# Eight experts in a two-layer MLP on one core: taking the layers two experts at a time, and storing one result in thirteen small transfers

## The chip, the core and the metric

The kernel runs on one core of one Trainium2 chip. The core has a matrix engine (TensorE, "PE" in the profile, with a weight-load side "PEld"), a vector engine (VectorE, "DVE"), a scalar engine (ScalarE, "ACT"), GpSimd ("POOL") and a sync engine ("SP"). Sixteen DMA engines move data between the chip's main memory (HBM) and the core's on-chip memories; transfers can be issued from POOL (they run in the queue that the profile calls q0) or from SP (q1). The metric is the device time of one execution in microseconds (us), smaller being better. The profile is of one execution; the times are those of several.

## The reference

```
x  : 8 experts x 256 rows x 512          (float32)
w1 : 8 experts x 512 x 2048
w2 : 8 experts x 2048 x 512

h   = relu(x @ w1)        # per expert, 256 x 2048
out = h @ w2              # per expert, 256 x 512, float32
```

There are 64 MiB of float32 weights, each used once; x and the result have 4 MiB each.

## The kernel before

The program is written by hand, engine by engine; each engine runs its own list in order, and semaphores are the only order between engines.

**Loads.** POOL issues the weight loads (`load_w1`, `load_w2`), which turn float32 into bf16 on the way. One load brings a whole weight matrix of one expert, 2 MiB as bf16. There are two buffers for each layer, `w1_sb[e % 2]` and `w2_sb[e % 2]`; a load into a buffer waits until TensorE is through with the expert two before (`s_h` counts blocks of the first layer, `s_o` output halves of the second). The order in the queue is w1(0), half of x, w2(0), w1(1), w2(1), w1(2), w2(2) and so on. The last, w2(7), goes in two parts: the first 9 of its 16 chunks (`CUT = 9`) and then the other 7. The other half of x comes by SP in four transfers.

**The start.** ACT and DVE cast and reorder x, TensorE transposes it, ACT and DVE copy the result out, and DVE gives each expert its 256 columns in one of two buffers `xe` (`give_xe`).

**An expert.** The first layer is four blocks (`q`) of 16 matmuls (L230) of 256 columns into two PSUM buffers `ph`; ACT takes the even blocks and DVE the odd ones, applying relu and writing `ht` in bf16 (L188, L200). The second layer is 32 matmuls of 512 columns (L247): 16 chunks (`kt`) for each of the two halves of the result, into `po[0]` and `po[1]`. DVE and ACT copy one half each to `o_sb` (L204, L190). There is one pair of `po`. TensorE's loop of four turns holds two experts, each with its first layer and then its second.

**Signals to TensorE.** SP waits for every weight load in the order of the queue and then adds to `t_w`, from which TensorE takes one at the head of each layer, and one at chunk 9 of the second (L98 to L103).

**Stores.** The result is stored at the end of the queues. Behind all weights POOL issues results 0 to 2 in one transfer (L146) and result 3 in three, of 36, 36 and 56 partitions (L149, `CUTS`). A partition of one result is 4 KB in one piece, here called a row; a result has 128 rows. SP, having waited for the last weight (L103), issues results 4 to 6 in one transfer (L106), waits for the last two copies, and issues result 7 (L109).

Of the kernel before, what the change touches and what calls it, by code (L numbers as in the profile page):

```python
# [9 lines left out]
def kernel(  # L10
# [7 lines left out]
    nc = tc.nc  # L18
    P = 128
    bf = mybir.dt.bfloat16  # L20
    f32 = mybir.dt.float32
    relu = mybir.ActivationFunctionType.Relu

    E, C, H = x.shape
    F = w1.shape[2]
    MT = C // P
    KT1 = H // P
    KT2 = F // P
    FB = 4
    NQ = KT2 // FB  # L30
    G = E // 2
    J = G * MT
    KH = KT1 // 2
    CUT = 9
    CUTS = (0, 36, 72, 128)

    w1_r = w1.rearrange("e (p kt) n -> e p kt n", p=P)
    w2_r = w2.rearrange("e (p kt) n -> e p kt n", p=P)
    out_r = out.rearrange("e (p mt) n -> p e mt n", p=P)
# [6 lines left out]
    x_f = nc.alloc_sbuf_tensor("x_f", [P, J, H], f32)  # L46
    x_c = nc.alloc_sbuf_tensor("x_c", [P, J, H], bf)
    x_b = nc.alloc_sbuf_tensor("x_b", [P, J, KH, P], bf)
    xt = [nc.alloc_sbuf_tensor(f"xt{g}", [P, KT1, MT, G * P], bf) for g in range(2)]
    xe = [nc.alloc_sbuf_tensor(f"xe{b}", [P, KT1, MT, P], bf) for b in range(2)]  # L50
    w1_sb = [nc.alloc_sbuf_tensor(f"w1_sb{b}", [P, KT1, F], bf) for b in range(2)]
    w2_sb = [nc.alloc_sbuf_tensor(f"w2_sb{b}", [P, KT2, H], bf) for b in range(2)]
    ht = [nc.alloc_sbuf_tensor(f"ht_sb{b}", [P, KT2, C], bf) for b in range(2)]
    o_sb = nc.alloc_sbuf_tensor("out_sb", [P, E, MT, H], f32)
    identity = nc.alloc_sbuf_tensor("identity", [P, P], bf)
    ph = [nc.alloc_psum_tensor(f"pt_h{b}", [P, FB, C], f32) for b in range(2)]
    po = [nc.alloc_psum_tensor(f"pt_o{m}", [P, H], f32) for m in range(MT)]
    pt = [nc.alloc_psum_tensor(f"pt_tr{b}", [P, J, P], bf) for b in range(2)]

    sem = nc.alloc_semaphore  # L60
    s_x = [sem(f"s_x{g}") for g in range(2)]
    s_out = [sem(f"s_out{i}") for i in range(3)]


    def load_x(e):
        nc.sync.dma_start(
            x_f[:, e * MT:(e + 1) * MT], x[e].rearrange("(p m) k -> p m k", m=MT)
        ).then_inc(s_x[0], 16)

    with tc.tile_critical(no_gpsimd_drain=True):  # L70
        for e in range(G // 2):
            load_x(e)
    tc.close()
    tc.compile()  # L74

    s_w1 = [sem(f"s_w1_{e}") for e in range(E)]
    s_w2 = [sem(f"s_w2_{e}") for e in range(E)]
    s_w2b = sem("s_w2b")
    s_id = sem("s_id")
    s_act = sem("s_act")  # L80
    s_dve = sem("s_dve")
    s_tr = sem("s_tr")
    s_h = sem("s_h")
    s_o = sem("s_o")
    t_xb = sem("t_xb")
    t_pt = [sem(f"t_pt{b}") for b in range(2)]
    t_xe = sem("t_xe")
    t_w = sem("t_w")
    t_ha = sem("t_ha")
    t_hb = sem("t_hb")  # L90

    sp, pool, act, dve, pe = nc.sync, nc.gpsimd, nc.scalar, nc.vector, nc.tensor


    for e in range(G // 2, G):
        load_x(e)
    for e in range(E):
        sp.wait_ge(s_w1[e], 16).then_inc(t_w, 1)  # L98
        if e < E - 1:
            sp.wait_ge(s_w2[e], 16).then_inc(t_w, 2)  # L100
        else:
            sp.wait_ge(s_w2[e], 16).then_inc(t_w, 1)
            sp.wait_ge(s_w2b, 16).then_inc(t_w, 1)  # L103
    sp.wait_ge(s_act, E - 1)
    sp.wait_ge(s_dve, E - 1)
    sp.dma_start(out_r[:, G:E - 1], o_sb[:, G:E - 1]).then_inc(s_out[1], 16)  # L106
# [5 lines left out]
    def load_w1(e):  # L112
        pool.dma_start(w1_sb[e % 2][:], w1_r[e]).then_inc(s_w1[e], 16)  # L113

    def load_w2(e):
        if e < E - 1:
            pool.dma_start(w2_sb[e % 2][:], w2_r[e]).then_inc(s_w2[e], 16)  # L117
        else:
            b = w2_sb[e % 2]
            pool.dma_start(b[:, :CUT], w2_r[e, :, :CUT]).then_inc(s_w2[e], 16)  # L120
            pool.dma_start(b[:, CUT:], w2_r[e, :, CUT:]).then_inc(s_w2b, 16)

    load_w1(0)
    pool.dma_start(x_c[:], x_rows).then_inc(s_x[1], 16)
    load_w2(0)
    pool.memset(identity[:], 0.0).then_inc(s_id, 1)
    pool.wait_ge(s_id, 1)
    pool.affine_select(
# [5 lines left out]
        pattern=[[-1, P]],  # L134
        channel_multiplier=1,
    ).then_inc(s_id, 1)
    load_w1(1)
    load_w2(1)
    for e in range(2, E):
        pool.wait_ge(s_h, NQ * (e - 1))  # L140
        load_w1(e)
        pool.wait_ge(s_o, MT * (e - 1))
        load_w2(e)
    pool.wait_ge(s_act, G)
    pool.wait_ge(s_dve, G)
    pool.dma_start(out_r[:, :G - 1], o_sb[:, :G - 1]).then_inc(s_out[0], 16)  # L146

    for p0, p1 in zip(CUTS, CUTS[1:]):
        pool.dma_start(out_r[p0:p1, G - 1], o_sb[p0:p1, G - 1]).then_inc(s_out[0], 16)  # L149
    pool.drain()  # L150


    def take_x(eng, half):

        js = slice(half * J // 2, (half + 1) * J // 2)
        copy = act.copy if eng is act else dve.tensor_copy
        for g, src in enumerate((x_f, x_c)):
            eng.wait_ge(s_x[g], 16 * (1 if g else G))  # L160
            for k in range(0, KT1, KH):
                r = (g * KT1 + k) // KH
                if r:
                    eng.wait_ge(s_tr, KH * r)
                copy(  # L165
                    x_b[:, js],
                    src[:, js].rearrange("p j (q t) -> p j t q", t=KT1)[:, :, k:k + KH],
                ).then_inc(t_xb, 1)
                eng.wait_ge(s_tr, KH * r + half + 1)
                copy(  # L170
                    xt[g][:, k + half].rearrange(
                        "p m (q l) -> p l m q" if g else "p m (l q) -> p l m q", l=G
                    ),
                    pt[half][:].rearrange("p (l m) q -> p l m q", m=MT),
                ).then_inc(t_pt[half], 1)

    def give_xe(e):
        g, i0 = e // G, (e % G) * P
        dve.tensor_copy(xe[e % 2][:], xt[g][:, :, :, i0:i0 + P]).then_inc(t_xe, 1)  # L179


    take_x(act, 1)
    s_xt = sem("s_xt")
    act.drain().then_inc(s_xt, 1)  # L184
    for e in range(E):
        for q in range(0, NQ, 2):
            act.wait_ge(s_h, NQ * e + q + 1)
            act.activation(ht[e % 2][:, FB * q:FB * (q + 1), :], ph[0][:], relu).then_inc(t_ha, 1)  # L188
        act.wait_ge(s_o, MT * e + 2)
        act.copy(o_sb[:, e, 1, :], po[1][:]).then_inc(s_act, 1)  # L190


    take_x(dve, 0)
    dve.wait_ge(s_xt, 1)
    give_xe(0)
    give_xe(1)
    for e in range(E):
        for q in range(1, NQ, 2):
            dve.wait_ge(s_h, NQ * e + q + 1)
            dve.tensor_relu(ht[e % 2][:, FB * q:FB * (q + 1), :], ph[1][:]).then_inc(t_hb, 1)  # L200
        if e + 2 < E:
            give_xe(e + 2)
        dve.wait_ge(s_o, MT * e + 1)
        dve.tensor_copy(o_sb[:, e, 0, :], po[0][:]).then_inc(s_dve, 1)  # L204


    def take(s, n=1):
        pe.wait_ge(s, n).then_inc(s, -n)  # L208

    pe.wait_ge(s_id, 2)  # L210
    for b in range(2):
        pe.sem_inc(t_pt[b], 1)
    with pe.Fori(0, 2 * KT1 // KH) as _r:
        take(t_xb, 2)
        for k in range(KH):
            take(t_pt[k])
            for j in range(J):
                ins = pe.transpose(pt[k][:, j], x_b[:, j, k], identity[:])  # L218
            ins.then_inc(s_tr, 1)

    with pe.Fori(0, E // 2) as _i:
        for b in range(2):
            take(t_xe)
            take(t_w)
            for q in range(NQ):
                if q >= 2:
                    pe.wait_ge((t_ha, t_hb)[q % 2], 1)
                for i in range(FB):
                    for kt in range(KT1):
                        ins = pe.matmul(  # L230
                            ph[q % 2][:, i, :],
                            w1_sb[b][:, kt, FB * q + i::KT2],
                            xe[b][:, kt],
                            start=(kt == 0),
                            stop=(kt == KT1 - 1),
                        )
                ins.then_inc(s_h, 1)
            take(t_w)
            for kt in range(KT2):
                if kt == 2 * FB:  # L240
                    take(t_ha, 2)
                if kt == 3 * FB:
                    take(t_hb, 2)
                if kt == CUT:
                    take(t_w)
                for m in range(MT):
                    ins = pe.matmul(  # L247
                        po[m][:],
                        ht[b][:, kt, m * P:(m + 1) * P],
                        w2_sb[b][:, kt, :],  # L250
                        start=(kt == 0),
                        stop=(kt == KT2 - 1),
                    )
                    if kt == KT2 - 1:
                        ins.then_inc(s_o, 1)

    sp.wait_ge(s_out[0], 16 * len(CUTS))
    sp.wait_ge(s_out[1], 16)
    sp.wait_ge(s_out[2], 16)


# [28 lines left out]
```

## Time and profile before

| | |
|---|---|
| median of 3 runs | 180.74 us (180.54 to 181.12) |
| the profiled execution: its time | 181.59 us |
| its span, from first to last instruction | 180.2 us |
| TensorE matmuls busy | 128.8 us (71%) |
| DVE, ACT busy | 37.5 us, 35.1 us |
| read from HBM, written to it | 71.30 MB, 4.19 MB |
| packets of the queue q0 (POOL), as a share of 16 engines' span | 93.5% |
| packets of the queue q1 (SP) | 5.9% |

The two lines on queues say how long the sixteen DMA engines were in packets of that queue, as a share of sixteen times the span. In a table of stretches ("windows") the DMA share is the same for one stretch, and GB/s counts the bytes as written: a weight that arrives as bf16 counts half of what was read for it. A result is float32 on both sides. The profile does not tell the sixteen engines apart.

### The profile page before, as it was taken

How to read it: one execution, taken by the hardware profiler on the slowest of the kernel's cores; microseconds unless marked ns; L12 is line 12 of the kernel's file. 1: busy time of each engine (PE TensorE's matmuls, PEld its weight loads, DVE VectorE, ACT ScalarE, POOL GpSimd, SP SyncE). 2: the span in 40 equal slices, each digit the busy share in tenths (PEclk: the TensorE clock that was granted, in tenths of full speed). 3: DMA queues.
4: the chain of work that ended last, by engine and by line, in shares of the span. 5: the costliest groups of instructions: out<-in, count | busy, mean ns of one | idle time of the engine just before them, and what ended most of it. 6: DMA issues, size and time to landing. Idle time of an engine off the chain costs nothing. (4 is left out here: it accounts for less than half of the span.)

```text
span 180.2 us, 1914 instructions
## 1 busy us (share of the span) xinstructions
PE 128.8 (71%) x824; PEld 92.4 (51%) x832; DVE 37.5 (21%) x40; ACT 35.1 (19%) x33; POOL 12.7 (7%) x28
## 2 busy tenths in 40 slices
PE   0004443299999999977979497949495997859990
PEld 0003333179479569526943485429341793359630
DVE  0023144602312312310231023012301022102210
ACT  2025536522014013010400022012201130102200
POOL 3400000000110110110010101010104300000000
PEclk9999999999999999996999879999999699988997
DMA  5989999998999999899989999998999999899995
GB/s 196 377 186 215 244 207 204 229 229 189 225 229 204 207 229 229 189 225 229 222 189 229 233 200 211 229 225 185 233 229 204 207 229 225 185 225 179 334 419 243
DMA packets 4321, 40.91 MB, mean 227 GB/s; under 512 B 480, under 2 KB 480, under 8 KB 2144
## 3 DMA queue, kind: packets, MB, share of 16 engines
q0 software_dynamic: 3200, 36.70, 93.5%
q1 hardware_dynamic: 1120, 4.19, 5.9%
q8 instruction: 1, 0.02, 0.0%
HBM read 71.30 MB, written 4.19 MB: 419 GB/s over the span
## 5 line engine op out<-in xcount | busy, mean ns | idle before, releaser
L230 PE MATMUL pt_h<-xe,w_sb 128*128 128x256 bf16 x512 | 66.8, 299 | 15.9 <-PEq L208 15.9
L230 PEld LDWEIGHTS pt_h<-xe,w_sb 128*128 128x128 bf16 x512 | 61.2, 148 | 23.0 <-issue 18.4
L247 PE MATMUL pt_o<-w_sb,ht_sb 128*128 128x512 bf16 x248 | 54.8, 379 | 6.1 <-PEq L208 5.9
L247 PEld LDWEIGHTS pt_o<-w_sb,ht_sb 128*128 128x128 bf16 x256 | 24.8, 98 | 34.2 <-issue 5.9
L200 DVE TENSOR_SCALAR ht_sb<-pt_h 128x1024 bf16<-128x1024 f32 x16 | 19.6, 1224 | 66.0 <-PE pt_h L230 66.0
L188 ACT ACTIVATE ht_sb<-pt_h 128x1024 bf16<-128x1024 f32 x16 | 16.4, 1023 | 53.7 <-PE pt_h L230 53.7
L218 PE MATMUL pt_tr<-identity,x_b 128*128 128x128 bf16 x64 | 7.5, 310 | 24.5 <-PEq L208 24.5
L218 PEld LDWEIGHTS pt_tr<-identity,x_b 128*128 128x128 bf16 x64 | 6.5, 144 | 25.2 <-issue 25.2
L190 ACT COPY out_sb<-pt_o 128x512 f32<-128x512 f32 x8 | 4.7, 588 | 66.7 <-PE pt_o L247 66.7
L204 DVE COPY out_sb<-pt_o 128x512 f32<-128x512 f32 x8 | 5.5, 691 | 47.4 <-PE pt_o L247 47.4
L113 POOL DMA_DIRECT2D w_sb<-in_w_dram x8 | 4.4, 554 | 85.0 <-PE pt_h L230 82.0
L170 ACT COPY xt<-pt_tr 128x1024 bf16<-128x1024 bf16 x4 | 6.9, 1720 | 8.8 <-PE pt_tr L218 8.8
L170 DVE COPY xt<-pt_tr 128x1024 bf16<-128x1024 bf16 x4 | 6.2, 1558 | 9.8 <-PE pt_tr L218 9.8
L117 POOL DMA_DIRECT2D w_sb<-in_w_dram x7 | 3.7, 536 | 33.9 <-PE pt_o L247 33.9
L165 ACT CAST x_b<-x_f 128x1024 bf16<-128x1024 f32 x2 | 4.0, 1997 | 8.2 <-DMA x_f<-in_x_dram 8.2
L165 DVE CAST x_b<-x_f 128x1024 bf16<-128x1024 f32 x2 | 2.1, 1074 | 12.4 <-DMA x_f<-in_x_dram 12.3
L179 DVE COPY xe<-xt 128x1024 bf16<-128x1024 bf16 x8 | 3.3, 418 | 0.9 <-ACTq L184 0.9
L165 ACT COPY x_b<-x_c 128x1024 bf16<-128x1024 bf16 x2 | 2.3, 1132 | 0.6 <-DMA x_c<-in_x_dram 0.6
L165 ACT ACT_TABLE_LOAD x1 | 1.3, 1283 | 2.8 <-PEq L74 2.8
L165 DVE COPY x_b<-x_c 128x1024 bf16<-128x1024 bf16 x2 | 1.4, 703 | 1.8 <-DMA x_c<-in_x_dram 1.8
L149 POOL DMA_DIRECT2D out_dram<-out_sb x3 | 1.6, 528 | 0.0
L120 POOL DMA_DIRECT2D w_sb<-in_w_dram x1 | 0.5, 531 | 9.0 <-PE pt_o L247 9.0
(9 smaller groups left out, 2.8 us busy)
## 6 DMA issues: line engine op xcount, KB each, us to landing
w_sb<-in_w_dram POOLq DMA_DIRECT2D x15, 2048.0 KB, 29.4
x_f<-in_x_dram SPq DMA_DIRECT2D x4, 512.0 KB, 4.3
out_dram<-out_sb POOLq DMA_DIRECT2D x1, 1536.0 KB, 33.8
out_dram<-out_sb SPq DMA_DIRECT2D x1, 1536.0 KB, 8.9
w_sb<-in_w_dram POOLq DMA_DIRECT2D x1, 1152.0 KB, 27.0
x_c<-in_x_dram POOLq DMA_DIRECT2D x1, 1024.0 KB, 19.2
w_sb<-in_w_dram POOLq DMA_DIRECT2D x1, 896.0 KB, 31.5
out_dram<-out_sb SPq DMA_DIRECT2D x1, 512.0 KB, 4.3
```

The source lines that it names most:

```text
L113: pool.dma_start(w1_sb[e % 2][:], w1_r[e]).then_inc(s_w1[e], 16)
L117: pool.dma_start(w2_sb[e % 2][:], w2_r[e]).then_inc(s_w2[e], 16)
L165: copy(x_b[:, js], src[:, js].rearrange("p j (q t) -> p j t q", t=KT1)[:, :, k:k + KH],).then_inc(t_xb, 1)
L170: copy(xt[g][:, k + half].rearrange("p m (q l) -> p l m q" if g else "p m (l q) -> p l m q", l=G), pt[half][:].rearrange("p (l m) q -> p l ...
L179: dve.tensor_copy(xe[e % 2][:], xt[g][:, :, :, i0:i0 + P]).then_inc(t_xe, 1)
L188: act.activation(ht[e % 2][:, FB * q:FB * (q + 1), :], ph[0][:], relu).then_inc(t_ha, 1)
L190: act.copy(o_sb[:, e, 1, :], po[1][:]).then_inc(s_act, 1)
L200: dve.tensor_relu(ht[e % 2][:, FB * q:FB * (q + 1), :], ph[1][:]).then_inc(t_hb, 1)
L204: dve.tensor_copy(o_sb[:, e, 0, :], po[0][:]).then_inc(s_dve, 1)
L218: ins = pe.transpose(pt[k][:, j], x_b[:, j, k], identity[:])
L230: ins = pe.matmul(ph[q % 2][:, i, :], w1_sb[b][:, kt, FB * q + i::KT2], xe[b][:, kt], start=(kt == 0), stop=(kt == KT1 - 1),)
L247: ins = pe.matmul(po[m][:], ht[b][:, kt, m * P:(m + 1) * P], w2_sb[b][:, kt, :], start=(kt == 0), stop=(kt == KT2 - 1),)
```

## The change

TensorE's loop still has two experts in a turn, but does both first layers and then both second layers. All lists follow it:

- POOL's queue holds w1(0), half of x, w1(1), w2(0), w2(1), and then for each pair w1, w1, w2, w2. The waits before a load are for the same events of the same expert as before.
- SP's list waits for w1 and w1, then w2 and w2. Between the two second layers of a pair it also waits for the copies of the first one's result (`s_act`, `s_dve`) before it signals the second one's weights, since there is one pair of `po`. The readiness of `xe` is also waited for here rather than by TensorE.
- ACT and DVE do the relus of both experts and then the two copies.
- TensorE takes `t_ha` and `t_hb` one by one, at blocks of the first layers and in the pair's last second layer.
- Result 3 is stored in thirteen transfers of 16, 15, 14, 13, 12, 11, 10, 9, 8, 7, 6, 5 and 2 rows in place of three of 36, 36 and 56.

Its core as a diff (the move of some definitions is left out):

```diff
-    CUTS = (0, 36, 72, 128)
+    ROWS = (16, 15, 14, 13, 12, 11, 10, 9, 8, 7, 6, 5, 2)
...
-    for e in range(E):
-        sp.wait_ge(s_w1[e], 16).then_inc(t_w, 1)
-        if e < E - 1:
-            sp.wait_ge(s_w2[e], 16).then_inc(t_w, 2)
-        else:
-            sp.wait_ge(s_w2[e], 16).then_inc(t_w, 1)
-            sp.wait_ge(s_w2b, 16).then_inc(t_w, 1)
+    for e in range(0, E, 2):
+        for b in range(2):
+            sp.wait_ge(s_xe, e + b + 1)
+            sp.wait_ge(s_w1[e + b], 16).then_inc(t_w, 1)
+        for b in range(2):
+            if b:
+                sp.wait_ge(s_act, e + 1)
+                sp.wait_ge(s_dve, e + 1)
+            if e + b < E - 1:
+                sp.wait_ge(s_w2[e + b], 16).then_inc(t_w, b + 1)
+            else:
+                sp.wait_ge(s_w2[e + b], 16).then_inc(t_w, 1)
+                sp.wait_ge(s_w2b, 16).then_inc(t_w, 1)
...
-    load_w2(0)
+    load_w1(1)
...
-    load_w1(1)
+    load_w2(0)
     load_w2(1)
-    for e in range(2, E):
-        pool.wait_ge(s_h, NQ * (e - 1))
-        load_w1(e)
-        pool.wait_ge(s_o, MT * (e - 1))
-        load_w2(e)
+    for e in range(2, E, 2):
+        for b in range(2):
+            pool.wait_ge(s_h, NQ * (e + b - 1))
+            load_w1(e + b)
+        for b in range(2):
+            pool.wait_ge(s_o, MT * (e + b - 1))
+            load_w2(e + b)
...
-    for p0, p1 in zip(CUTS, CUTS[1:]):
-        pool.dma_start(out_r[p0:p1, G - 1], o_sb[p0:p1, G - 1]).then_inc(s_out[0], 16)
+    p0 = 0
+    for n in ROWS:
+        pool.dma_start(out_r[p0:p0 + n, G - 1], o_sb[p0:p0 + n, G - 1]).then_inc(s_out[0], 16)
+        p0 += n
...
     with pe.Fori(0, E // 2) as _i:
         for b in range(2):
-            take(t_xe)
             take(t_w)
             for q in range(NQ):
-                if q >= 2:
-                    pe.wait_ge((t_ha, t_hb)[q % 2], 1)
+                if b or q >= 2:
+                    take((t_ha, t_hb)[q % 2])
...
+        for b in range(2):
             take(t_w)
             for kt in range(KT2):
-                if kt == 2 * FB:
-                    take(t_ha, 2)
-                if kt == 3 * FB:
-                    take(t_hb, 2)
-                if kt == CUT:
+                if b and kt == 2 * FB:
+                    take(t_ha)
+                if b and kt == 3 * FB:
+                    take(t_hb)
+                if b and kt == CUT:
                     take(t_w)
```

More of the change, by code (lines that the diff above doesn't have):

```diff
@@ L62 @@
     s_out = [sem(f"s_out{i}") for i in range(3)]
[L65 to L74, printed above, removed]
     s_w1 = [sem(f"s_w1_{e}") for e in range(E)]
@@ L92, with take, load_x @@
     sp, pool, act, dve, pe = nc.sync, nc.gpsimd, nc.scalar, nc.vector, nc.tensor
+    def take(s, n=1):
+        pe.wait_ge(s, n).then_inc(s, -n)
+    def load_x(e):
+        sp.dma_start(
+            x_f[:, e * MT:(e + 1) * MT], x[e].rearrange("(p m) k -> p m k", m=MT)
+        ).then_inc(s_x[0], 16)
+    with tc.tile_critical(no_gpsimd_drain=True):
+        for e in range(G // 2):
+            load_x(e)
+    tc.close()
+    tc.compile()
     for e in range(G // 2, G):
         load_x(e)
-    for e in range(E):
-        sp.wait_ge(s_w1[e], 16).then_inc(t_w, 1)
-        if e < E - 1:
-            sp.wait_ge(s_w2[e], 16).then_inc(t_w, 2)
-        else:
-            sp.wait_ge(s_w2[e], 16).then_inc(t_w, 1)
-            sp.wait_ge(s_w2b, 16).then_inc(t_w, 1)
+    for e in range(0, E, 2):
[11 more added lines that the diff above has]
+                sp.wait_ge(s_w2b, 16).then_inc(t_w, 1)
     sp.wait_ge(s_act, E - 1)
@@ L184 @@
     act.drain().then_inc(s_xt, 1)
[L185 to L190, printed above, removed]
+    for e in range(0, E, 2):
+        for b in range(2):
+            for q in range(0, NQ, 2):
+                act.wait_ge(s_h, NQ * (e + b) + q + 1)
+                act.activation(ht[b][:, FB * q:FB * (q + 1), :], ph[0][:], relu).then_inc(t_ha, 1)
+        for b in range(2):
+            act.wait_ge(s_o, MT * (e + b) + 2)
+            act.copy(o_sb[:, e + b, 1, :], po[1][:]).then_inc(s_act, 1)
+    dve.sem_inc(t_pt[0], 1)
     take_x(dve, 0)
@@ L196 @@
     give_xe(1)
[L197 to L208, printed above, removed]
+    for e in range(0, E, 2):
+        for b in range(2):
+            for q in range(1, NQ, 2):
+                dve.wait_ge(s_h, NQ * (e + b) + q + 1)
+                dve.tensor_relu(ht[b][:, FB * q:FB * (q + 1), :], ph[1][:]).then_inc(t_hb, 1)
+            if e + 2 < E:
+                give_xe(e + b + 2)
+        for b in range(2):
+            dve.wait_ge(s_o, MT * (e + b) + 1)
+            dve.tensor_copy(o_sb[:, e + b, 0, :], po[0][:]).then_inc(s_dve, 1)
     pe.wait_ge(s_id, 2)
-    for b in range(2):
-        pe.sem_inc(t_pt[b], 1)
     with pe.Fori(0, 2 * KT1 // KH) as _r:
@@ L237 @@
                 ins.then_inc(s_h, 1)
+        for b in range(2):
             take(t_w)
             for kt in range(KT2):
-                if kt == 2 * FB:
-                    take(t_ha, 2)
-                if kt == 3 * FB:
-                    take(t_hb, 2)
-                if kt == CUT:
+                if b and kt == 2 * FB:
[3 more added lines that the diff above has]
+                if b and kt == CUT:
                     take(t_w)
@@ L255 @@
                         ins.then_inc(s_o, 1)
-    sp.wait_ge(s_out[0], 16 * len(CUTS))
-    sp.wait_ge(s_out[1], 16)
-    sp.wait_ge(s_out[2], 16)
+    for s, n in zip(s_out, (1 + len(ROWS), 1, 1)):
+        sp.wait_ge(s, 16 * n)
 _INS = ['x', 'w1', 'w2']
```

5 lines of the change are left out of this document (3 added, 2 removed).

## The prediction

> **What bounds the kernel now.** I read the page first, then the chain of waits, SP's waits, then stretches of time. The chain that ended last names only TensorE, from w1(7)'s landing to the last copy. It stops where the last store is issued, and doesn't say who sets that landing or the store's.
>
> ```profile
> span 180.2 us, 1914 instructions
> PE 128.8 (71%) x824; PEld 92.4 (51%) x832; DVE 37.5 (21%) x40; ACT 35.1 (19%) x33; POOL 12.7 (7%) x28
> 159.54 8.85 PE pt_h L230 x64
> 168.44 6.87 PE pt_o L247 x31
> 175.33 0.58 ACT out_sb L190
> HBM read 71.30 MB, written 4.19 MB: 419 GB/s over the span
> ```
>
> SP's own queue tells more: it waits for weights nearly all the time. The stretch behind it shows the DMA engines full from the first weight to the last part of w2(7).
>
> ```profile
> SPq L98 <- DMA w_sb<-in_w_dram: 82.4, 8, 14.7
> SPq L100 <- DMA w_sb<-in_w_dram: 72.9, 7, 14.5
> L98 SPq EVENT_SEMAPHORE  x8: 17/17/17, 18.4 to 159.4; - x8
> L100 SPq EVENT_SEMAPHORE  x7: 17/17/17, 32.9 to 149.7; - x7
> L103 SPq EVENT_SEMAPHORE  x1: 17/17/17, 169.9 to 169.9; - x1
> core 0: us, PE busy (x), PEclk, DMA share, GB/s
> 18.40:166.00 147.60, 117.66 (x757) 0.95 1.02 216
> ```
>
> From w2(0) at 32.9 to w1(7) at 159.4 thirteen loads land, one per (159.4 − 32.9) / 13 = 9.73 us, with a DMA share of 1.02. A layer takes TensorE 7 to 9 us, so TensorE waits for data. The end is a second stage, of 4.19 MB of results:
>
> ```profile
> core 0: us, PE busy (x) PEld busy (x) DVE busy (x) ACT busy (x) POOL busy (x), PEclk, DMA share, GB/s
> 169.60:175.80 6.20, 5.69 (x27) 2.37 (x25) 0.73 (x2) 0.47 (x1) 0.00 (x0) 1.00 1.03 419
> 176.40:177.00 0.60, 0.00 (x0) 0.00 (x0) 0.00 (x0) 0.00 (x0) 0.00 (x0) 1.00 0.87 355
> 177.00:177.60 0.60, 0.00 (x0) 0.00 (x0) 0.00 (x0) 0.00 (x0) 0.00 (x0) 1.00 1.01 410
> 178.20:178.70 0.50, 0.00 (x0) 0.00 (x0) 0.00 (x0) 0.00 (x0) 0.00 (x0) 0.50 0.51 205
> 179.00:179.40 0.40, 0.00 (x0) 0.00 (x0) 0.00 (x0) 0.00 (x0) 0.00 (x0) 0.50 0.07 31
> 179.40:179.80 0.40, 0.00 (x0) 0.00 (x0) 0.00 (x0) 0.00 (x0) 0.00 (x0) 0.50 0.05 20
> 175.94 0.35 SPq L109 DMA_DIRECT2D out_dram<-out_sb  x1
> out_dram<-out_sb SPq DMA_DIRECT2D x1, 512.0 KB, 4.3
> ```
>
> The last column but one is the important one. Until 178 the engines are full, apart from a short dip before result 7 arrives; from 179.0 to 179.8 the share is 0.05 to 0.07, and 0.07 × 16 is one engine. So **one DMA engine finishes about 1 us behind the other fifteen, and it alone sets the end.** Its work can be counted. Sixteen engines at 419 GB/s move a 4 KB row in 4096 × 16 / 419 = 156 ns each. The last weight landed at 169.9 and result 7 at 175.94 + 4.3 = 180.2. If the same engine was last both times, it moved 10.3 / 0.156 = 66 rows between. Seven full results give each engine 128 / 16 = 8 rows, 56 in all. The other 10 are rows of result 3, of which a fair share would be 8. That fits blocks of ⌈36/16⌉ + ⌈36/16⌉ + ⌈56/16⌉ = 3 + 3 + 4.
>
> The profiled execution took 181.59 us, 1.4 more than its span and 0.85 over the median of 180.74. I sum differences against its span and put them on the median.
>
> **The change part by part.** *Order of the loads: 0.* The queue carries the same 17 loads and the same x, in another order, so the stream ends at 169.9 if it never runs dry. In slots of 9.73 us the new order lands w1(1) at 32.9, w2(0) 42.6, w2(1) 52.4, w1(2) 62.1, w1(3) 71.8, w2(2) 81.5, w2(3) 91.3. The buffers come free as TensorE goes:
>
> ```profile
> 35.24 10.02 PE L230 MATMUL pt_h<-xe,w_sb 128*128 128x256 bf16 x64 [3.25 <-PEq L208]
> 45.31 6.85 PE L247 MATMUL pt_o<-w_sb,ht_sb 128*128 128x512 bf16 x31
> 52.00 7.15 PE L230 MATMUL pt_h<-xe,w_sb 128*128 128x256 bf16 x64
> 45.55 0.53 POOL L113 DMA_DIRECT2D w_sb<-in_w_dram  x1 [38.48 <-PE pt_h L230]
> ```
>
> First layer 0 ends at 45.3 as before, and w1(2) is issued at 45.55, 6.9 us before the queue empties. First layer 1 then ends at 52.5 (w1(3) issued 9.6 us early), second layer 0 at 59.4 (w2(2), 12 us early), second layer 1 at 67 (w2(3), 14 us early); later ones are earlier still. Without that cover each microsecond of lateness costs one.
>
> *The wait for the copies between second layers: 0.* It holds TensorE and, on SP's list, the signals behind it. Copies need 0.65 us (the last matmul ends at 168.44 + 6.85 = 175.29, the store is issued at 175.94), and from landing to matmul it takes 159.54 − 159.4 = 0.15: 0.8 us per pair. For three pairs TensorE waits for weights anyway. At the end:
>
> ```profile
> 120.79 7.18 PE L230 MATMUL pt_h<-xe,w_sb 128*128 128x256 bf16 x64 [2.64 <-PEq L208]
> 159.54 8.85 PE L230 MATMUL pt_h<-xe,w_sb 128*128 128x256 bf16 x64 [2.65 <-PEq L208]
> L102 SPq EVENT_SEMAPHORE  x1: 17/17/17, 164.9 to 164.9; - x1
> 159.50:164.00 4.50, 4.46 (x26) 3.72 (x27) 0.00 (x0) 1.02 (x1) 0.00 (x0) 0.62 0.99 205
> ```
>
> Second layer 6 starts at 159.5 in the slot that w1(7) had. It takes 6.85 us, or up to 8.55 where the granted clock is down for a while, as in the 0.62 of the last row (8.85 against 7.18 for one layer after equal waits). So it ends at 166.4 to 168.1, second layer 7 runs from 167.2–168.9 to 174.0–175.8 (its first part landed at 164.9 and its rest at 169.9, both in time), and result 7 is issued at 174.7 to 176.4 instead of 175.94. **That earlier issue is worth nothing:** the last engine has 58 other rows to move first and comes to result 7 only at about 179.8 − 8 × 0.156 = 178.6. It costs nothing either until the issue passes 177.5, since a transfer reaches the engines 1.1 us after issue (175.94 to the end of the dip at 177.0).
>
> *Thirteen transfers: the rows.* Dealt in blocks from the first place on, one row per engine, the stair gives places 0 to 15 of the engines 13, 13, 12, 12, 12, 11, 10, 9, 8, 7, 6, 5, 4, 3, 2 and 1 rows. Before, it was 10 rows for places 0 to 11, 4 for two and none for two. The late engine is one of the twelve; which, no view tells. Over the twelve the new mean is 118 / 12 = 9.8 rows: −0.03 us. The ends are place 0, 3 × 0.156 = +0.47, and place 11, −0.78, of which some −0.6 counts, because engines of place 0 or 1 with 3 rows more then end last.
>
> The Trainium skill ("DMA: Bandwidth & Descriptors", section "Why a DMA increments its semaphore by 16 and not by 1") says that some copies issued from GpSimd give each engine the partitions divided by 16, rounded up, from engine 0 on; the count of 10 agrees. The same page ("Latency and other measured facts") says that engines 7 and 15 are usually slower: 15 had no rows here, so it would be 7, with 9 rows, −0.16 us, and a sum of 180.7 where the mean place gives 180.8.
>
> *Thirteen transfers: their number.* POOL issues ten more:
>
> ```profile
> 138.87 0.76 POOL L146 DMA_DIRECT2D out_dram<-out_sb  x1
> 139.61 1.56 POOL L149 DMA_DIRECT2D out_dram<-out_sb  x3
> out_dram<-out_sb POOLq DMA_DIRECT2D x1, 1536.0 KB, 33.8
> out_dram<-out_sb POOLq DMA_DIRECT2D x2, 144.0 KB, 33.4
> ```
>
> At 1.56 / 3 = 0.52 us each they occupy POOL from about 139.6 to 146.4, with nothing behind them and 25 us before the data can move. In the engines each transfer has a completion. From 169.6 to 175.8 some four fell on each engine and cost at most (430 − 419) / 430 × 6.2 = 0.16 us, if 430 is the full rate (216 in the weights' stretch, read at twice that). So ten more cost 0 to 0.4. I take 0.05, near zero, as the share of 1.03 shows no gap.
>
> *The rest: 0.* The move of `xe`'s wait to SP adds at most 0.15 us to the first layer 0, against 6.9 of cover. TensorE's new waits for relus at the second first layer find them done: the slower relu takes 1.22 us, a block 7.15 / 4 = 1.8.
>
> ```profile
> L200 DVE TENSOR_SCALAR ht_sb<-pt_h 128x1024 bf16<-128x1024 f32 x16 | 19.6, 1224 | 66.0 <-PE pt_h L230 66.0
> ```
>
> Sum: 0 + 0 − 0.03 + 0.05, or −0.11 at the skill's place. I forecast **180.7 us, no change**.
>
> **The rivals.**
> 1. *The late engine gets far fewer rows:* a place from 9 on, or a dealing in rotation (8 rows each). −0.3 to −0.6 us: 180.1 to 180.4. For it: the stair falls along the places. Against: no view shows the place.
> 2. *It gets more, or it isn't the bound without the profiler.* At place 0 or 1, or if the lag is under 4 × 0.156 = 0.6 us in ordinary executions, 13 rows end last: +0.3 to +0.6, 181.2. For it: the profiled execution is 0.85 us slower than the median.
> 3. *Result 7 comes too late (slower).* If the clock is down in both last second layers, layer 7 ends at 177.5 and the issue is at 178.1, 0.6 past the turning point of 177.5: 181.3 us. Against: the row 168.44 6.87 ran at full clock, and the gap before layer 7 is only 0.8 us.
> 4. *Each small transfer pays its own fixed time.* Result 7 alone took 4.3 us, of which 8 × 0.156 = 1.25 is rows; ten times the other 3.05 would be +30 us, 211. Against: the two transfers of 144 KB were issued 0.52 us apart and, after 33.4 us each, landed 0.5 apart: 3 rows are 0.47, so completions overlap. The Trainium skill (the same page, "Rules for kernel authors") speaks for it: transfers under 64 KB are mostly overhead; 4 to 64 KB each is what we have here. These rows disagree for queued transfers.
> 5. *The stream runs dry after the swap:* only if first layer 0 ends after about 51 us: +1 us for each one late, 181.7 or more.
>
> **How the numbers follow.** Forecast 0.52, with its own range 180.3 to 181.1. Rival 1: 0.18. Rival 2: 0.12. Rival 3: 0.08. Rival 4: 0.03. Rival 5: 0.04. Another lag of the late engine, either sign: 0.03. The range 179.9 to 181.6 takes in rivals 1 to 3 and leaves out about 1 in 10. About 0.3% (0.54 us) is what a measurement of this kernel can tell from no change. Below 180.2: most of rival 1, 0.17. Above 181.28: most of 2, all of 3 to 5, 0.25. Between: 0.58.
>
> **What would show it.** The last part of w2(7) still lands at 169.9 ± 0.3; the DMA share stays at 1.0 up to there. Second layer 7 starts 0.8 us behind layer 6 and ends at 174 to 176. The last stretch still has a tail of share 0.06, one engine, as long as now within 0.3 us. The prediction is wrong if that tail is gone or doubled, if the weights end elsewhere, or if result 7 is issued after 177.5.

## The result, and the profile after

| | before | changed |
|---|---|---|
| median of 18 runs each | 181.18 us | 181.87 us |
| lowest, highest | 180.48, 182.20 | 181.32, 183.30 |
| ratio, with its 95% interval | | 1.0049 (1.0031 to 1.0067) |

The change made the kernel slower by 0.5%: about 0.9 us by the ratio, 0.7 between the two medians. I had forecast no change, and the median lies above my range (179.9 to 181.6). Part of the distance is the base: the forecast stood on a median of 180.74, and these eighteen runs of the kernel before gave 181.18. But 180.74 × 1.0049 = 181.6 also is the upper end of the range and not 180.7. The profiled execution of the changed kernel is no slower than that of before, so a single trace can't carry the verdict here: the changed kernel's 18 spans lie between 179.8 and 182.0 us, and the profiled one is the shortest. From the page of the changed kernel:

```profile
span 179.8 us, 1940 instructions
DMA packets 4529, 40.91 MB, mean 228 GB/s; under 512 B 688, under 2 KB 688, under 8 KB 2352
L160 POOL DMA_DIRECT2D out_dram<-out_sb x13 | 6.5, 505 | 0.0
```

The 688 packets under 512 B are 208 more than before (480). Ten more transfers have 160 completions. The other 48 fit the dealing in blocks that the prediction assumed, with one small packet for each row that an engine has less than the fullest: 80 in the stair, 12 + 12 + 8 = 32 with 36, 36 and 56 rows. Up to the last weight all is as foreseen. These are TensorE's last two stretches, SP's wait for the last part of w2(7), the issue of result 7, and the stretch of the weights:

```profile
159.56 7.07 PE L260 MATMUL pt_o<-w_sb,ht_sb 128*128 128x512 bf16 x32 [0.69 <-PEq L82]
167.41 7.07 PE L260 MATMUL pt_o<-w_sb,ht_sb 128*128 128x512 bf16 x32 [0.79 <-PEq L82]
L112 SPq EVENT_SEMAPHORE  x1: 17/17/17, 169.6 to 169.6; - x1
175.13 0.35 SPq L118 DMA_DIRECT2D out_dram<-out_sb  x1
18.40:166.00 147.60, 117.91 (x782) 84.78 (x783) 33.26 (x35) 27.76 (x27) 14.06 (x27) 0.97 1.02 216
```

The weights land at 169.6 with the DMA share at 1.02, the gap between the second layers is 0.79 us, and result 7 is issued at 175.13. The difference is in the stretch of the stores. The columns of these tables of stretches are the stretch, its length, the busy time of PE, PEld, DVE, ACT and POOL, the clock, the DMA share and GB/s. First the kernel before, then the changed one:

```profile
172.00:175.00 3.00, 3.00 (x16) 1.27 (x13) 0.00 (x0) 0.00 (x0) 0.00 (x0) 1.00 1.03 419
175.00:178.00 3.00, 0.29 (x2) 0.00 (x0) 0.69 (x1) 0.58 (x1) 0.00 (x0) 0.94 0.98 401
178.00:179.00 1.00, 0.00 (x0) 0.00 (x0) 0.00 (x0) 0.00 (x0) 0.00 (x0) 0.50 0.46 184
178.70:179.00 0.30, 0.00 (x0) 0.00 (x0) 0.00 (x0) 0.00 (x0) 0.00 (x0) 0.50 0.07 27
```

```profile
172.00:175.00 3.00, 2.48 (x12) 0.91 (x10) 0.69 (x1) 0.48 (x1) 0.00 (x0) 1.00 1.05 368
175.00:178.00 3.00, 0.00 (x0) 0.00 (x0) 0.00 (x0) 0.10 (x1) 0.00 (x0) 1.00 1.02 416
178.00:179.00 1.00, 0.00 (x0) 0.00 (x0) 0.00 (x0) 0.00 (x0) 0.00 (x0) 0.73 0.56 225
178.70:179.00 0.30, 0.00 (x0) 0.00 (x0) 0.00 (x0) 0.00 (x0) 0.00 (x0) 0.50 0.24 96
```

From 172 to 175 the engines count as fully busy in both (1.03 and 1.05), but move 368 GB/s instead of 419: packets take longer. That is (419 − 368) / 419 × 3 = 0.37 us lost by the average engine. At the end, 178.7 to 179.0, a share of 0.24 is four engines, where the kernel before had one (0.07): the tail of one engine, which I had expected to stay, is gone. From the last weight at 169.6 to the landing of result 7 at 175.13 + 4.6 = 179.7 are 10.1 us, 65 rows' time instead of 66, lengthened packets included. So if the same engine is late, it has no more rows than before; the others have come up to it.

### The profile page after: what moved, and what is told of

It reads as the page before. It is cut to its first block, busy times and chain, and to the rows that moved or that the text cites. A ratio compares the mean times of both kernels' runs of the same rounds, so it can differ in the third digit from the quotient of the medians.

```text
span 179.8 us, 1940 instructions
## 1 busy us (share of the span) xinstructions
PE 127.5 (71%) x832; PEld 89.5 (50%) x832; DVE 37.5 (21%) x40; ACT 35.1 (20%) x33; POOL 17.6 (10%) x38
## 5 line engine op out<-in xcount | busy, mean ns | idle before, releaser
L242 PE MATMUL pt_h<-xe,w_sb 128*128 128x256 bf16 x512 | 60.4, 282 | 12.0 <-PEq L82 12.0
L260 PE MATMUL pt_o<-w_sb,ht_sb 128*128 128x512 bf16 x256 | 59.9, 395 | 10.5 <-PEq L82 10.5
L242 PEld LDWEIGHTS pt_h<-xe,w_sb 128*128 128x128 bf16 x512 | 57.7, 146 | 15.4 <-issue 13.6
L260 PEld LDWEIGHTS pt_o<-w_sb,ht_sb 128*128 128x128 bf16 x256 | 25.4, 101 | 43.9 <-issue 17.5
L160 POOL DMA_DIRECT2D out_dram<-out_sb x13 | 6.5, 505 | 0.0
```

What stands on the lines that cost most here:

```text
L160: pool.dma_start(out_r[p0:p0 + n, G - 1], o_sb[p0:p0 + n, G - 1]).then_inc(s_out[0], 16)
L242: ins = pe.matmul(ph[q % 2][:, i, :], w1_sb[b][:, kt, FB * q + i::KT2], xe[b][:, kt], start=(kt == 0), stop=(kt == KT1 - 1),)
L260: ins = pe.matmul(po[m][:], ht[b][:, kt, m * P:(m + 1) * P], w2_sb[b][:, kt, :], start=(kt == 0), stop=(kt == KT2 - 1),)
```

## The experiments

Each kernel was timed against the kernel before on its own chip. All ratios, in the order of the runs:

| kernel | order of layers | result 3 in | median us | ratio to before (95%) |
|---|---|---|---|---|
| rows_only | as before | stair | 181.83 | 1.0056 (1.0035 to 1.0077) |
| pairs_cuts | pairs | 36, 36, 56 | 180.98 | 1.0010 (0.9987 to 1.0033) |
| old_one | as before | 128 | 181.18 | 1.0025 (1.0003 to 1.0047) |
| pairs_one | pairs | 128 | 180.80 | 1.0005 (0.9981 to 1.0029) |
| pairs_16x8 | pairs | 8 of 16 | 181.10 | 1.0012 (0.9983 to 1.0041) |
| pairs_32x4 | pairs | 4 of 32 | 181.00 | 1.0017 (0.9982 to 1.0051) |
| pairs_16s8 | pairs | 8 of 16, every eighth row | 181.49 | 1.0024 (0.9994 to 1.0053) |
| pairs_sems | pairs | stair, own semaphores | 181.46 | 1.0044 (1.0016 to 1.0071) |
| pairs_17 | pairs | 5 of 17, one of 43 | 181.39 | 1.0034 (1.0016 to 1.0052) |
| pairs_32c | pairs | 8 of 16, and results 0 to 2 too | 181.13 | 1.0017 (1.0000 to 1.0035) |
| pairs_stair | pairs | stair (the changed kernel) | 181.93 | 1.0069 (1.0044 to 1.0094) |
| pairs_cuts2 | pairs | 36, 36, 56 | 180.81 | 0.9994 (0.9973 to 1.0014) |
| pairs_spread | pairs | stair, every fourth row | 181.07 | 1.0011 (0.9992 to 1.0030) |
| pairs_stair2 | pairs | stair (the changed kernel) | 181.67 | 1.0038 (1.0019 to 1.0058) |
| spread_sbuf | pairs | stair, reads spread | 181.33 | 1.0026 (1.0003 to 1.0049) |
| spread_hbm | pairs | stair, writes spread | 181.38 | 1.0017 (0.9995 to 1.0039) |

"Stair" is the thirteen sizes of the change. The first eight rows come from one chip, the next four from a second, the two after them from a third and the last two from a fourth; across chips only the ratios compare.

**Which half of the change costs.** Four kernels: one half alone each, and both orders with a single transfer for result 3.

```diff
 # rows_only: the kernel before, with only this
-    for p0, p1 in zip(CUTS, CUTS[1:]):
-        pool.dma_start(out_r[p0:p1, G - 1], o_sb[p0:p1, G - 1]).then_inc(s_out[0], 16)
+    for n in ROWS:
+        pool.dma_start(out_r[p0:p0 + n, G - 1], o_sb[p0:p0 + n, G - 1]).then_inc(s_out[0], 16)
+        p0 += n
 # pairs_cuts: the changed kernel, with only this
-    ROWS = (16, 15, 14, 13, 12, 11, 10, 9, 8, 7, 6, 5, 2)
+    ROWS = (36, 36, 56)
 # old_one and pairs_one: the two, with
+    ROWS = (128,)
```

rows_only:

> The order of loads and layers as before; result 3 in the thirteen transfers. Theory A (the stair is the cost: the engines at places 0 and 1 carry 13 rows instead of 10 and end last in executions where no other engine lags by a microsecond): +0.6 to +1.0 us, ratio 1.003 to 1.006. Theory B (the order by pairs is the cost, the stair is neutral): within 0.2 us, ratio 0.999 to 1.001. Theory C (each half of the two): +0.3 to +0.5 us.

pairs_cuts:

> The order by pairs; result 3 in three transfers of 36, 36 and 56 rows as before. Theory A: within 0.2 us of the kernel before, ratio 0.999 to 1.001. Theory B: +0.6 to +1.0 us, ratio 1.003 to 1.006, with result 7 issued or the last weight landing later than before in the trace. Theory C: +0.3 to +0.5 us.

old_one:

> The order as before; result 3 in one transfer of 128 rows, 8 rows for each engine, one completion. If a single late engine with 10 rows of result 3 sets the end in most executions (the prediction's reading), it has two rows less and the time falls by 0.2 to 0.4 us, ratio 0.998 to 0.999. If the late engine is one that had no rows of result 3 before, it has eight more and the time rises by 0.5 to 1.2 us.

pairs_one:

> The order by pairs; result 3 in one transfer of 128 rows. Theory A: the same as the one-transfer kernel in the old order, within 0.2 us, and below the changed kernel by 0.6 to 1.2 us. Theory B: 0.6 to 1.0 us above the one-transfer kernel in the old order.

The stair alone gives the whole loss, 1.0056, and the order by pairs none, 1.0010 and in a second measurement 0.9994. Theory B and theory C fall. The stretches of the stair alone, and then of the pairs with three transfers:

```profile
172.00:175.00 3.00, 1.51 (x7) 0.49 (x5) 0.69 (x1) 0.58 (x1) 0.00 (x0) 1.00 1.04 349
175.00:178.00 3.00, 0.00 (x0) 0.00 (x0) 0.00 (x0) 0.00 (x0) 0.00 (x0) 0.59 1.02 415
178.00:179.00 1.00, 0.00 (x0) 0.00 (x0) 0.00 (x0) 0.00 (x0) 0.00 (x0) 0.50 0.54 221
179.00:180.30 1.30, 0.00 (x0) 0.00 (x0) 0.00 (x0) 0.00 (x0) 0.00 (x0) 0.50 0.09 35
```

```profile
172.00:175.00 3.00, 2.68 (x13) 1.00 (x11) 0.50 (x1) 0.28 (x1) 0.00 (x0) 1.00 1.04 423
175.00:178.00 3.00, 0.00 (x0) 0.00 (x0) 0.19 (x1) 0.30 (x1) 0.00 (x0) 0.85 0.98 400
178.00:179.00 1.00, 0.00 (x0) 0.00 (x0) 0.00 (x0) 0.00 (x0) 0.00 (x0) 0.50 0.20 82
```

The slow stretch goes with the stair and not with the order: 349 against 423 GB/s. In rows_only the share from 179.0 to 180.3 is 0.09, 0.09 × 16 × 1.3 = 1.9 us of engine time: two engines, not one, were at work to the end. The single transfer gave no gain in the old order, against its expectation of 0.2 to 0.4 us less: its interval lies above 1, and why is open. With pairs it is even with the kernel before.

The trace holds the duration of every packet. A row's packet takes 159 ns. Counted over all packets of rows after 167 us, one profiled execution each:

```
kernel         packets over 175 ns   time above 159 ns, summed
before                  0                   0.28 us
pairs_cuts              0                   0.32 us
pairs_cuts2             2                   0.30 us
old_one, pairs_one      0                   0.21 us
pairs_16s8              4                   0.72 us
pairs_16x8              9                   1.65 us
pairs_32x4              7                   2.02 us
pairs_17               21                   4.47 us
pairs_spread           18                   4.51 us
spread_sbuf            18                   4.54 us
pairs_32c             102                   5.03 us
changed kernel         20                   5.52 us
rows_only              29                   7.56 us
pairs_stair            20                   7.92 us
pairs_sems             28                   8.15 us
pairs_stair2           36                   9.27 us
spread_hbm             38                   9.87 us
```

With the stair, 20 to 36 single packets stall. They mostly take 200 to 800 ns, and they start between 171.5 and 176, about the stretch in which the stair is stored (171.7 to 175.3). The added time divided by sixteen is 0.35 to 0.58 us an engine, close to what the missing rate gives (0.37 to 0.59). Many of the stalled packets are not the stair's own: 17 of the 20 in the changed kernel, and 13 to 18 in each of the other traces of the stair, belong to results 4 to 6, which come from SP at the same time.

**What makes the packets stall.** Even shares with more completions, the same with other rows, and the stair with a semaphore for each transfer:

```diff
 # pairs_16x8, pairs_32x4: the changed kernel with
+    ROWS = (16,) * 8           # or (32,) * 4
 # pairs_16s8: eight transfers of every eighth row
+    for j in range(8):
+        pool.dma_start(out_r[j::8, G - 1], o_sb[j::8, G - 1]).then_inc(s_out[0], 16)
 # pairs_sems: the stair, each transfer with a semaphore of its own
+        pool.dma_start(out_r[p0:p0 + n, G - 1], o_sb[p0:p0 + n, G - 1]).then_inc(s_row[i], 16)
```

pairs_16x8:

> The order by pairs; result 3 in eight transfers of 16 neighbouring rows, so that each engine has 8 rows of one 4 KB row each and eight completions. Theory S (the shares: 13 rows at the first places end last): the shares are even, so within 0.2 us of the one-transfer kernel by pairs. Theory N (many short transfers stall the engines: one row per completion): the rate falls from about 420 to 360-390 GB/s between 172 and 174 in the trace, and the time rises by 0.3 to 0.6 us over the one-transfer kernel.

pairs_32x4:

> The order by pairs; result 3 in four transfers of 32 rows: even shares, two rows per completion. Theory S: as the one-transfer kernel. Theory N: between the one-transfer kernel and the eight transfers, under 0.3 us over the former, the rate between 172 and 175 at 400 GB/s or more.

pairs_16s8:

> The order by pairs; eight transfers of 16 rows as in the kernel of eight neighbouring-row transfers, but each takes every eighth row, so that an engine's rows are those that it has in the one transfer of 128. Theory N: the same stalls as with neighbouring rows. Theory P (sixteen engines at neighbouring rows get in each other's way): no stalls, rate 410 to 430 GB/s between 172 and 175, time as the one-transfer kernel. Theory S: as the one-transfer kernel.

pairs_sems:

> The changed kernel, with a semaphore of its own for each of the thirteen transfers. Theory C (some two hundred completions on one semaphore within 2 us get in each other's way): the stalls go, rate back to 410-430 GB/s between 172 and 175, and the time falls by 0.3 to 0.7 us against the changed kernel. Theories S, N and P: no difference to the changed kernel, 0.4 to 0.9 us over the kernel before.

Theory C falls: with thirteen semaphores the rate from 172 to 175 is 346 GB/s and the time stays at 1.0044. With even shares the rate is 407 (16x8), 403 (32x4) and 410 (16s8), there are few stalls, and the ratios of 1.0012 to 1.0024 can't be told from 1 or from each other. So in the traces one row per completion does not make the stair's slow stretch. The times are less clear: pairs_16s8, which theory P had expected at the time of the single transfer, has a median of 181.49, as high as the stair in pairs_sems (181.46) and 0.7 above pairs_one on the same chip. Its interval takes in both no loss and the stair's.

**Shares without many transfers, and many transfers without shares.**

```diff
 # pairs_17: by blocks rounded up, 13 rows each for places 0 to 7, in six transfers
+    ROWS = (17, 17, 17, 17, 17, 43)
 # pairs_32c: results 0 to 3 in eight transfers each, 32 completions, even shares
+    for e in range(G):
+        for p0 in range(0, P, 16):
+            pool.dma_start(out_r[p0:p0 + 16, e], o_sb[p0:p0 + 16, e]).then_inc(s_res[e], 16)
```

pairs_17:

> The order by pairs; result 3 in six transfers of 17, 17, 17, 17, 17 and 43 rows. By blocks rounded up this gives places 0 to 7 thirteen rows each, place 8 eight, and the others one to three: the stair's heaviest share on eight engines with few completions. Theory S (the shares): at least as slow as the stair, +0.5 to +1.0 us over the three transfers by pairs, and in the trace eight or more engines land result 7 late. Theory N (the number of short transfers): at most 0.3 us over the three transfers by pairs.

pairs_32c:

> The order by pairs; results 0 to 3 each in eight transfers of 16 rows: even shares, and 32 completions on each engine instead of 14 in the stair. Theory N: slower than the stair, +0.8 us or more over the three transfers by pairs, the rate below 400 GB/s from 168 to 175. Theory S: within 0.3 us of the three transfers by pairs.

pairs_stair:

> The changed kernel once more, on the same chip as the two kernels above: ratio 1.003 to 1.007, packets stalled between 172 and 175.

pairs_cuts2:

> The three transfers of 36, 36 and 56 rows with the order by pairs once more, on the same chip: ratio 0.999 to 1.002, no stalled packets.

On one chip: three transfers 0.9994, 32 completions 1.0017, heavy shares 1.0034, the stair 1.0069. The number alone gives a small part: 32 transfers of 64 KB cost about 0.4 us against three (the intervals overlap), not the 0.8 or more that theory N asked for, though they slow the stretch as a whole (its rate from 172 to 175):

```profile
172.00:175.00 3.00, 2.47 (x12) 0.92 (x10) 0.69 (x1) 0.49 (x1) 0.00 (x0) 1.00 1.02 381
178.00:179.00 1.00, 0.00 (x0) 0.00 (x0) 0.00 (x0) 0.00 (x0) 0.00 (x0) 0.51 0.24 94
179.00:180.30 1.30, 0.00 (x0) 0.00 (x0) 0.00 (x0) 0.00 (x0) 0.00 (x0) 0.50 0.00 0
```

Here 102 packets are longer, half of them by under 40 ns, and little of it is seen at the end: nothing runs after 179. The uneven shares of pairs_17 cost 0.7 us over the three transfers with far fewer transfers, as theory S had it, and they come with 21 stalls too. Whether that is less than the stair's loss can't be told, as the two intervals overlap. How many engines end late in pairs_17 its trace can't say: in that execution (182.97 us) result 7 was issued at 178.10 only. So neither theory is shown to give the whole loss alone.

**The same shares, other rows.** The stair takes neighbouring rows, so up to sixteen engines read neighbouring partitions at once. Here each transfer takes every fourth row; two more kernels spread only the reading or only the writing side, and so store result 3 with its rows in another order.

```diff
 # pairs_spread: sizes and their order as in the stair; four classes of every fourth row
+        j = GROUP[n]            # (16, 14, 2), (15, 12, 5), (13, 11, 8), (10, 9, 7, 6)
+        p0 = j + 4 * done[j]
+        p1 = min(p0 + 4 * n, P)
+        pool.dma_start(out_r[p0:p1:4, G - 1], o_sb[p0:p1:4, G - 1]).then_inc(s_out[0], 16)
 # spread_sbuf
+        pool.dma_start(out_r[r0 - n:r0, G - 1], o_sb[p0:p1:4, G - 1]).then_inc(s_out[0], 16)
 # spread_hbm
+        pool.dma_start(out_r[p0:p1:4, G - 1], o_sb[r0 - n:r0, G - 1]).then_inc(s_out[0], 16)
```

pairs_spread:

> The changed kernel with the same thirteen sizes in the same order, so the same shares for each engine and the same number of completions, but each transfer takes every fourth row of the result instead of neighbouring rows. Theory P (the stalled packets come from many engines at neighbouring rows, and the stalls are most of the loss): stalls gone, rate 410 GB/s or more from 172 to 175, ratio 0.999 to 1.003. Theory S (the shares are most of the loss, the stalls add little): stalls gone or not, ratio 1.003 to 1.006. If the stalls stay, their cause is the number of short or empty shares and not the rows' places.

pairs_stair2:

> The changed kernel on the same chip, as the base for the spread rows: ratio 1.004 to 1.007, 20 or more stalled packets, rate 350 to 390 GB/s from 172 to 175.

spread_sbuf:

> As the kernel with spread rows, but only the reading side is spread: each of the thirteen transfers reads every fourth partition on the chip and writes neighbouring rows of the result in HBM. Result 3 is so stored with its rows permuted, which is the part of the computation that this kernel changes; sizes, shares and bytes are the stair's. If many engines at neighbouring partitions on the chip are in each other's way, this is as fast as the spread rows (ratio 0.999 to 1.003, under 20 stalled packets); if the places in HBM matter, it is as slow as the stair (1.003 to 1.007).

spread_hbm:

> The mirror image: each of the thirteen transfers reads neighbouring partitions and writes every fourth row of result 3 in HBM, again with permuted rows in result 3 as the changed part. If the reading side is the cause, as slow as the stair (1.003 to 1.007, rate 340 to 370 GB/s from 172 to 175); if the writing side is, as fast as the spread rows (0.999 to 1.003).

The first row below is the stair, then come the spread rows, both on one chip. The reading side alone and then the writing side alone ran on another chip, where the stair itself was not run. Each is shown from 172 to 175:

```profile
172.00:175.00 3.00, 3.00 (x16) 1.37 (x14) 0.00 (x0) 0.00 (x0) 0.00 (x0) 1.00 1.04 336
```

```profile
172.00:175.00 3.00, 2.39 (x12) 0.88 (x9) 0.69 (x1) 0.57 (x1) 0.00 (x0) 1.00 1.03 369
178.00:179.00 1.00, 0.00 (x0) 0.00 (x0) 0.00 (x0) 0.00 (x0) 0.00 (x0) 1.00 0.32 127
```

```profile
172.00:175.00 3.00, 2.46 (x12) 0.90 (x10) 0.69 (x1) 0.50 (x1) 0.00 (x0) 1.00 1.04 374
```

```profile
172.00:175.00 3.00, 2.47 (x12) 0.91 (x10) 0.69 (x1) 0.49 (x1) 0.00 (x0) 1.00 1.05 336
```

With spread rows the time is 181.07 us against 181.67 for the stair, 0.6 us less, with the same shares and the same number of transfers. So most of that chip's loss (0.86 us by the medians) went with the places of the rows. The two intervals overlap at their edges, but the twelve times of each hardly do: 180.63 to 181.40 against 181.08 to 181.96. The rate rises only from 336 to 369, and 18 stalls stay. In these traces the reading side makes the difference: spread reads give the rate and the 18 stalls of the spread rows, spread writes give 336 GB/s and 38 stalls as in the stair. By queue, the stair's own stalled packets fall from 19 to 2 with spread rows, and are 2 with spread reads and 23 with spread writes; those of SP's queue are 15 to 17 in all four. The times of the last two, 1.0026 and 1.0017, don't bear that out: they can't be told apart. Nor is the difference in rate beyond what traces of the stair show among themselves: the changed kernel's first trace had 368 GB/s, 20 stalls and 3 of its own. That neighbouring partitions are what stalls the reads is therefore supported by one trace each, and not shown in time.

**What stays open.** Shown: the stair is the whole loss; packets of its own and of SP's queue stall in it; the shared semaphore isn't why; and on one chip, with the same sizes on every fourth row, most of the loss is gone. Supported, with overlapping intervals: the number of transfers gives about a third of the loss on the chip that had both. Not settled: how the loss divides between stalls and the 13 rows of the first places, why neighbouring rows stall, and what the 16 packets of SP's queue that still stall with spread rows wait for. No tried version was faster than the kernel before beyond its interval; the pairs with three transfers or one are even with it.

## Why the prediction was wrong

**The bound: right, but read too strictly.** The stores end with a late engine in the trace of before, and it moved 66 rows, then 65. From "it alone sets the end" I gave the other engines a microsecond of room and counted their losses as free. That room was read from one execution. By the last completions of result 7 in the packet records, the late engine ends 1.08 us behind the next one there, but 0.66 and 0.60 in the two traces of the pairs with three transfers and 0.37 in pairs_one. In the changed kernel 0.28 us are left, and in rows_only two engines work to 180.

**Order of the loads, the wait for the copies: right.** 0 was the forecast for both, and pairs_cuts gives 1.0010 and 0.9994. The time of issue was foreseen as 174.7 or 176.4, according to the clock. The executions show both cases, 0.4 later each: 175.13 above, and 176.80 where layer 6 ran at the lower clock (8.75 us against 7.07), here in pairs_32x4:

```profile
159.54 8.75 PE L260 MATMUL pt_o<-w_sb,ht_sb 128*128 128x512 bf16 x32 [2.36 <-PEq L82]
169.09 7.07 PE L260 MATMUL pt_o<-w_sb,ht_sb 128*128 128x512 bf16 x32 [0.79 <-PEq L82]
176.80 0.35 SPq L118 DMA_DIRECT2D out_dram<-out_sb  x1
177.00:178.00 1.00, 0.00 (x0) 0.00 (x0) 0.00 (x0) 0.00 (x0) 0.00 (x0) 1.00 0.45 180
179.00:180.00 1.00, 0.00 (x0) 0.00 (x0) 0.00 (x0) 0.00 (x0) 0.00 (x0) 1.00 0.00 0
```

There the engines did run out of work (0.45 at 177 to 178), and the execution still ended by 179.5. The last completions of its sixteen engines lie between 178.93 and 179.09, so result 7 came just in time for the late engine. That the issue costs nothing holds at 176.80; that it would still hold at 177.5, no run shows.

**Thirteen transfers, the rows: the sign for the late engine was right, the weight wrong.** The term of −0.03, or −0.16 at place 7, went by the late engine alone. The first places' +0.47 stood in the text as an end of the range. It belongs in the sum as soon as the other terms use up the room of the other engines. Two figures beside it were off without changing the forecast: −0.11 gives 180.6, not 180.7; and rival 2's +0.3 to +0.6 lies mostly below 181.28, not above it.

**Thirteen transfers, their number: the step that failed.** I took 0.05 us, with 0.4 as the upper bound, from completions in the stretch of the kernel before, and left a row at its 0.156 us. The change cost 0.7 to 0.9 us. What I priced was a completion; what came was stalled packets: the rate fell from 419 to 368, 349 and 336 GB/s over 3 us, 0.37, 0.50 and 0.59 us for the average engine. The bound was taken from transfers of 3 or 4 rows for each of 12 to 14 engines, and nothing in that trace had single neighbouring rows for up to sixteen. I called the number the risk and put the rows' places at nothing; on the chip that had both, the same thirteen sizes on every fourth row lost 0.26 us by the medians in place of 0.86, so the places are the larger part there. Why neighbouring rows stall stays open.

**The rivals.** The nearest to what happened is rival 2, "13 rows end last", at 181.2 and a chance of 0.12; its sign and more than half of its size fit, and its mechanism is at most a part of the cause, which pairs_17 supports but doesn't show. Rival 1 had the sign wrong. Rival 4 was put at +30 us for serial fixed times. That is refuted. In the changed kernel the transfers were issued 0.505 us apart; this is the time to landing of the first, the twelfth and the thirteenth:

```profile
out_dram<-out_sb POOLq DMA_DIRECT2D x1, 64.0 KB, 31.3
out_dram<-out_sb POOLq DMA_DIRECT2D x1, 20.0 KB, 28.3
out_dram<-out_sb POOLq DMA_DIRECT2D x1, 8.0 KB, 30.2
```

The first twelve landed within 11 × 0.505 + 28.3 − 31.3 = 2.6 us, 0.23 for each; the last one followed after 0.505 + 30.2 − 28.3 = 2.4 us, so all thirteen took 5.0 us and not 30. And 32 transfers of 64 KB cost about 0.4 us. The transfers of the stair are of 8 to 64 KB, not 4 to 64. The Trainium skill ("DMA: Bandwidth & Descriptors", section "Rules for kernel authors") advises to join many small transfers into one large, as under 64 KB one pays mostly overhead. That direction holds here, on a much smaller scale. Rivals 3 and 5 were not seen in the traces of the changed kernel; the late issue of rival 3 came in one trace of another kernel, at 178.10 in pairs_17, where the weights landed at 171.2 in place of 169.6 and layer 6 ran at the lower clock (8.54 us).

## What to carry to other kernels

Where one late unit sets the end, work out the room that the others have, and add up all that the change takes from that room before any of it is counted as free. A price per transfer from one shape need not hold for another: with transfers of 2 to 16 neighbouring rows packets stalled that did not with 36. When an effect is as small as the spread of single executions, first find out with halves of the change which half it is, and only then read traces.

## What the runs showed of the hardware

- While engines stored single 4 KB rows of neighbouring partitions in thirteen transfers, 20 to 36 single packets took mostly 200 to 800 ns instead of 159, also those of another queue. The DMA share stayed at 1.04 to 1.06; only GB/s shows the loss.
- 32 queued 64 KB transfers ran at 381 GB/s from 172 to 175, against 419 with one large and three smaller transfers.
- By the packet records, the last of the sixteen engines is behind by a constant and not by more with each load. In the kernel before, its completions of the weight loads come 0.64 us behind the median engine's up to 42 us, and 1.15 us behind from 51 to 139 us; a packet of 16 KB from the instruction queue lies between, at 47.8 us. In the changed kernel it is 0.58 and then 1.18 us, with that packet at 52.6 us. That the packet causes the step was not tested, and in pairs_cuts the lag is 1.17 us from the first load on.
- Thirteen semaphores in place of one made no difference (346 against 336 to 368 GB/s).
